# A two-layer diffusion step on one core: gate blocks, final norm, first weights and operand placement

## The chip, the core and the metric

One core of a Trainium2 chip runs the whole program. The metric is the time of one execution in microseconds (us) on the device; lower is better. The five engines are PE (matrix multiply; its weight loads are listed as PEld), DVE (vector), ACT (scalar activations), POOL (GpSimd) and SP, which issues most DMAs here. Each engine runs its own instructions strictly in the written order and waits at semaphores for the others.

## The reference

Two token groups go through the same two layers: 256 latent tokens (conditioned by `c`, reading cached context keys and values) and 128 context tokens (conditioned by `c_ctx`). D is 1024, there are 8 heads of 128, and the FFN width is 2816. Everything is float32.

```python
def run_layer(x, cond, l, ctx_kv, use_rope):
    mod = silu(cond) @ w_mod[l] + b_mod[l]              # 9 vectors of 1024
    sh1, sc1, gt1, sh2, sc2, gt2, sh3, sc3, gt3 = split(mod, 9)
    h = rmsnorm(x, g_norm[l, 0]) * (1 + sc1) + sh1
    x = x + 0.5 * gt1 * swiglu(h, ffn1_w13[l], ffn1_w2[l])
    h = rmsnorm(x, g_norm[l, 1]) * (1 + sc2) + sh2
    m, k_state, v_state = mixer(h, l, ctx_kv, use_rope)
    x = x + gt2 * m
    h = rmsnorm(x, g_norm[l, 2]) * (1 + sc3) + sh3
    return x + 0.5 * gt3 * swiglu(h, ffn2_w13[l], ffn2_w2[l])

def mixer(h, l, ctx_kv, use_rope):
    z, q, k, v, gates = split(h @ w_in[l])
    u, vv = split(gelu(z))                              # gating unit
    a = u * (w_spatial[l] @ rmsnorm(vv, gain) + b_spatial[l])   # 128x128 mixing, 4 groups
    o = softmax(q1 k1) v - lam * softmax(q2 k2) v       # per head, rope on latents
    b = rmsnorm(o, subln_gain[l]) * (1 - lam_init)
    return (sigmoid(g_a) * (a @ w_branch_a) + sigmoid(g_b) * (b @ w_branch_b)) @ w_out

y = rmsnorm(x after two layers, g_final)                # for both groups
```

## The kernel before

All 384 tokens sit side by side in the free dimension: `x` is 128 partitions x 8 tiles (`dt`) x 384 tokens. A projection is computed as three matmuls per 128x128 weight tile (`mm3`, lines 233 to 235): weights and activations are each split into a rounded high part and the rest (`whi`/`wlo`, `S_hi`/`S_lo`), and hi*hi, lo*hi and hi*lo are added in PSUM. ACT writes the high part of each weight chunk of 128x1024 (line 181), DVE the low part (line 184); SP loads the chunks into seven `raw` buffers (line 150).

The order of the program is written by a small planner: a list of *jobs*, each consuming weight chunks in order. A *column job* (`col_job`) is 24 matmuls with 384 moving columns (386 where the un-normed `u` is used, whose last two columns carry the shift vector); a *token-major job* (`tokmajor_job`, lines 394 to 396) is 18 matmuls with 512 moving columns. At the start of every job with weights one entry of the list `bg` is run (`run_bg(1)`), and attention interleaves its phases with matmuls by the table `ORDER` (`F3` means three steps of a job, `X2` means phase x of the unit two back).

Three places are touched.

*The gate* (`push_sgu`, pushed just before the q and k jobs of head 0). `sgu_norm` computes 1/rms of the gated half (POOL does the power and the refinement steps), `sgu_scale(j)` scales token tile j (DVE, line 762), and `sgu_block(cb)` does three mixing matmuls (PE, line 773) into one PSUM tile `tp`, of which there is a single buffer, and then evacuates it on DVE and ACT (lines 777, 780, 414, 417). The next block's matmuls can start when line 777 has read `tp`. The jobs that follow are q0, k0 and eight token-major jobs for v (v0 to v7); with v0 to v3 go steps of the next modulation vectors, DVE work at lines 443, 445, 451 and 460.

*The start* (`start_group`). Before the first projection, layer 0's first shift and scale vectors are computed in four quarters: `products(q)` is 32 small matmuls (line 302), `finish(q)` two transposes (line 317) and a few DVE operations, after which `make(kt)` writes the normed activations of tiles 2q and 2q+1 (lines 556, 561, 564). `warm(n)` issues n matmuls on a tile of ones with no reader (line 336).

*The end*. After the last FFN, `update_x` (line 628) and `norm_sq` (lines 508, 509) finish the eighth tile of x, `norm_stats` sums squares on PE (line 532), `rsqrt` runs on POOL and DVE, `norm_bcast` spreads the result over partitions (lines 545 to 549), and eight DVE operations (line 1127) write y, each followed by a DMA from SP (line 1130).

Where the tiles lie: the allocator gives every tile a multiple of 32 bytes in each partition. In the built program before the change, `x`, `t`, `raw` and the activation slots S0 and S2 to S6 start 32 bytes past a multiple of 128, and S1, S7, all `whi` and `wlo` 96 bytes past one. A row of 384 numbers is 1536 bytes, 12 times 128; a row of `u` is 1544 bytes, so its eight rows start 8 bytes further along each time.

Of the kernel before, what the change touches and what calls it, by code (L numbers as in the profile page):

```python
# [26 lines left out]
RAW_BUFS = 7  # L27
PER_HEAD = 27
LO_LAG = 4
ORDER = [(c[0], int(c[1:])) for c in "S0 F1 B0 T1 F3 E0 C0 O2 F4 P1 F1 X2".split()]  # L30
W_BUFS = 4
WARM = (28, 5, 10)
TINY = {"yq": 2, "yv": 2, "ys": 2, "yl": 2, "yb": 3, "y2": 4, "yo": 4, "ye": 4, "yc": 4}

SH1, SC1, GT1, SH2, SC2, GT2, SH3, SC3, GT3 = range(9)
TOK = ((1, 0, 256), (0, 256, 384))
# [5 lines left out]
def hybrid_step(  # L42
# [29 lines left out]
    bmod = cp.tile([P, DEPTH, 9, KD], F32, name="bmod")  # L72
    gnorm = cp.tile([P, DEPTH, 3, KD], F32, name="gnorm")
    sgain = cp.tile([P, DEPTH, KD], F32, name="sgain")
    sublng = cp.tile([P, DEPTH], F32, name="sublng")
    gfin = cp.tile([P, KD], F32, name="gfin")
    neglam = cp.tile([P, DEPTH], F32, name="neglam")
    modT = cp.tile([P, DEPTH, 9, KD, 2], F32, name="modT")
    amod = cp.tile([P, 3, KD, 2], F32, name="amod")

# [207 lines left out]
    def start_group(keys, rhs, evacs, make):  # L288
# [42 lines left out]
        junk = pp.tile([P, P], F32, tag="tp", name="tp")  # L331

        def warm(n):

            for _ in range(n):
                T.matmul(junk, lhsT=ones, rhs=ones, start=True, stop=True)

        def gen(c):
            n = len(keys)
            nst["h"] = duo(role["Y"])  # L340
            warm(WARM[0])
            norm_stats()
            products(0)
            warm(WARM[1])
            norm_bcast()
            finish(0)
            warm(WARM[2])
            for i in range(2):
                split_upto(c + i)
                make(i)  # L350
                run_later(99)
            split_upto(c + n - 1)
            run_later(99)
            ws = [split_of.pop(c + i) for i in range(n)]
            pss = [ps_mm() for _ in range(n)]
            r_hi, r_lo = rhs()
            for q in range(4):
                seq = [(i, kt) for kt in (2 * q, 2 * q + 1) for i in range(n)]
                if q == 3:
                    seq = [(i, kt) for i in range(n) for kt in (6, 7)]  # L360
                for e, (i, kt) in enumerate(seq):
                    if q < 3 and e == (5, 1, 1)[q]:
                        products(q + 1)
                    if q < 3 and e == (7, 3, 3)[q]:
                        finish(q + 1)
                        make(2 * q + 2)
                        make(2 * q + 3)
                    sl = slice(kt * P, (kt + 1) * P)
                    hi, lo = ws[i]
                    mm3(pss[i][:, :NT], hi[:, sl], lo[:, sl], r_hi[:, kt, :], r_lo[:, kt, :], kt == 0, kt == KD - 1)  # L370
                    if kt == KD - 1:
                        evacs[i](pss[i][:, :NT])
# [218 lines left out]
    def make_u(l, i, kt):  # L591

        if kt == 0:
            nst["u"] = tuple(slot(2 * role["Y"] + n, [P, KD, NU], F32R) for n in range(2))
        u_hi, u_lo = nst["u"]
        for n, s0, s1 in TOK:
            S.activation(
# [28 lines left out]
    def update_x(l, pc, dt, ps, after):  # L626
        for n, s0, s1 in TOK:
            V.scalar_tensor_tensor(  # L628
                out=x[:, dt, s0:s1], in0=ps[:, s0:s1], scalar=modT[:, l, pc, dt, n:n + 1],
                in1=x[:, dt, s0:s1], op0=ALU.mult, op1=ALU.add)  # L630
        norm_sq(dt)
        if after is not None:
            make_u(*after, dt)


    def ffn(l, i, w13, w2, mods, after, n13):
# [83 lines left out]
    def mixer(l, mods, after):  # L720
# [362 lines left out]
    with tc.manual_schedule():  # L1083
# [39 lines left out]
        norm_stats()
        norm_bcast()
        y = slot(0, [P, KD, NT])
        for dt in range(KD):
            V.scalar_tensor_tensor(
                out=y[:, dt, :], in0=x[:, dt, :], scalar=gfin[:, dt:dt + 1], in1=nst["rb"],
                op0=ALU.mult, op1=ALU.mult)
            nc.sync.dma_start(out=a["y"][:, dt, :], in_=y[:, dt, :])  # L1130


# [77 lines left out]
```

## Time and profile before

| | |
|---|---|
| median of 3 runs | 1936.64 us (1936.42 to 1937.65) |
| profiled execution | 1935.43 us, of which the span from first to last instruction is 1933.7 us |
| PE busy | 1908.7 us, 99% of the span |
| matmuls at lines 233, 234 and 235 | 3136 each: 2816 with 384 columns, 320 with 386 |
| DVE, ACT, POOL busy | 1323.3, 795.2, 248.9 us |
| DMA | 308.71 MB, mean 160 GB/s |
| granted PE clock | 0.995 mean |

Times in the profile count from the span's start. In a row of the timeline the columns are: start in us, length in us, engine, line of the kernel, operation, output<-inputs, size, how many equal instructions the row merges, and in brackets how long the engine had been idle and who ended that. PE's pipelined matmuls overlap, so their lengths are latencies; the distance between starts is their rate. In the table of windows the columns are the stretch, its length, the busy time and number of instructions of each engine, the granted PE clock, the DMA share and GB/s.

### The profile page before, as it was taken

To read this page: it belongs to the slowest core of one execution; us is meant where nothing else is said; L and a number is where in the kernel's file an instruction comes from. 1 tells how busy PE (TensorE), PEld (TensorE's weight loads), DVE (VectorE), ACT (ScalarE), POOL (GpSimd) and SP (SyncE) were. 2 spreads that over 40 slices of the span, in tenths; PEclk is the share of its full clock that TensorE was granted. 3 is DMA by queue.
4 is the path that set the end of the run, shared out by engine and by line. 5 is a ranking of instruction groups with operands and counts; after the bars stand their busy time and mean duration, and the time that the engine had idled before them with its cause. 6 is when DMAs were issued, how large, how long until landed. Compare 5 with 4: busy or idle time off the path is not lost.

```text
span 1933.7 us, 28616 instructions
## 1 busy us (share of the span) xinstructions
PE 1908.7 (99%) x10992; PEld 1839.8 (95%) x10992; DVE 1323.3 (68%) x2016; ACT 795.2 (41%) x1435; POOL 248.9 (13%) x527
## 2 busy tenths in 40 slices
PE   8999999999999999999999999999999999999997
PEld 6999999878899999999999999998898999999997
DVE  4677885777666668778768779668677456655533
ACT  3433334536653344333334333344565534433321
POOL 0000003203431022000040000050134300400000
PEclk9999999999999999999999999999999999999998
DMA  8566664643334435566536556545333333354430
GB/s 312 198 196 200 215 210 131 208 144 110 99 100 156 151 115 190 192 199 214 197 99 222 196 191 226 171 136 191 121 103 97 113 120 124 115 172 157 153 109 34
DMA packets 92154, 308.71 MB, mean 160 GB/s; under 512 B 10864, under 2 KB 18416, under 8 KB 91248
## 3 DMA queue, kind: packets, MB, share of 16 engines
q1 hardware_dynamic: 91584, 306.76, 48.4%
q8 instruction: 87, 1.43, 0.3%
q14 instruction: 51, 0.42, 0.1%
q10 hardware_dynamic: 432, 0.11, 0.0%
HBM read 303.16 MB, written 3.67 MB: 159 GB/s over the span
## 4 chain that ended last, share of the span: by engine, by line
PE 82%; issue 13%; DVE 3%; POOL 1%; DMA 1%; ACT 1%; POOLq 0%; DVEq 0%; ACTq 0%
PE mm L233 24%; PE mm L234 23%; PE mm L235 23%; PE mm L394 2%; PE mm L396 2%; PE mm L395 2%; PE sc L943 2%; PE mm L992 1%; DVE wlo L184 1%; PE tp L976 1%; PE sc L302 0%; DMA S<-in_w_mod 0%; POOL t L578 0%; PE tp L773 0%; POOL t L576 0%
## 5 line engine op out<-in xcount | busy, mean ns | idle before, releaser
L233 PE MATMUL mm<-S,whi 128*128 128x384 f32 (+1 forms) x3136 | 1073.8, 342 | 2.3 <-ACT S L561 2.3
L234 PE MATMUL mm<-S,wlo 128*128 128x384 f32 (+1 forms) x3136 | 1053.5, 336 | 3.7 <-DVE wlo L184 3.6
L235 PE MATMUL mm<-S,whi 128*128 128x384 f32 (+1 forms) x3136 | 1050.7, 335 | 0.0
L184 DVE TENSOR_TENSOR wlo<-raw,whi 128x1024 fp32r<-128x1024 f32 x424 | 520.0, 1227 | 241.6 <-ACT whi L181 241.0
L233 PEld LDWEIGHTS mm<-S,whi 128*128 128x128 f32 x3136 | 589.9, 188 | 24.7 <-issue 18.7
L234 PEld LDWEIGHTS mm<-S,wlo 128*128 128x128 f32 x3136 | 588.6, 188 | 5.4 <-DVE wlo L184 5.1
L235 PEld LDWEIGHTS mm<-S,whi 128*128 128x128 f32 x3136 | 589.2, 188 | 0.4 <-DVE S L564 0.4
L181 ACT ACTIVATE whi<-raw 128x1024 fp32r<-128x1024 f32 x424 | 445.0, 1051 | 186.6 <-PE mm L235 112.8
L445 DVE SCALAR_TENSOR_TENSOR acc<-raw,scond,acc 128x1024 f32<-128x1024 f32 x224 | 277.1, 1278 | 0.0
L414 ACT ACTIVATE S<-t 128x384 fp32r<-128x384 f32 x144 | 73.9, 522 | 332.6 <-DVE t L672 241.2
L515 POOL TENSOR_TENSOR yr<-yv,nhalf 128x3 f32<-128x3 f32 x9 | 7.7, 856 | 1344.8 <-DVE yv L535 1269.8
L417 DVE TENSOR_TENSOR S<-t,S 128x384 fp32r<-128x384 f32 x144 | 83.7, 588 | 34.5 <-ACT S L414 34.5
L672 DVE TENSOR_TENSOR t<-t,mm 128x384 f32<-128x384 f32 x76 | 42.0, 553 | 77.9 <-PE mm L235 77.8
L653 ACT ACTIVATE t<-mm 128x384 f32<-128x384 f32 x76 | 37.3, 490 | 137.7 <-PE mm L235 137.7
L394 PE MATMUL mm<-whi,S 128*128 128x512 f32 x192 | 77.4, 403 | 0.0
L396 PE MATMUL mm<-whi,S 128*128 128x512 f32 x192 | 75.2, 392 | 0.0
L395 PE MATMUL mm<-wlo,S 128*128 128x512 f32 x192 | 75.1, 391 | 0.0
L508 ACT ACTIVATE t<-x 128x384 f32<-128x384 f32 x45 | 23.4, 524 | 109.5 <-DVE x L628 109.5
L578 POOL TENSOR_SCALAR t<-t,amod,modT 128x256 f32<-128x256 f32 x80 | 67.0, 846 | 4.2
L628 DVE SCALAR_TENSOR_TENSOR x<-mm,modT,x 128x256 f32<-128x256 f32 x96 | 35.5, 411 | 33.1 <-PE mm L235 32.9
L576 POOL TENSOR_TENSOR t<-x,rb 128x384 f32<-128x384 f32 x40 | 49.0, 1224 | 28.9 <-ACT rb L549 20.3
L955 ACT ACTIVATE e<-sc,ym 128x384 f32<-128x384 f32 (+1 forms) x96 | 47.9, 507 | 6.7 <-DVE ym L946 6.4
(138 smaller groups left out, 1189.1 us busy)
## 6 DMA issues: line engine op xcount, KB each, us to landing
raw<-in_ffn_w SPq DMA_DIRECT2D x264, 512.0 KB, 4.4
raw<-in_w_mod SPq DMA_DIRECT2D x132, 512.0 KB, 4.7
raw<-in_w_in SPq DMA_DIRECT2D x112, 512.0 KB, 3.9
raw<-in_w_branch_a SPq DMA_DIRECT2D x16, 512.0 KB, 3.6
raw<-in_w_branch_b SPq DMA_DIRECT2D x16, 512.0 KB, 3.7
raw<-in_w_out SPq DMA_DIRECT2D x16, 512.0 KB, 3.7
S<-in_w_mod SPq DMA_DIRECT2D x6, 1024.0 KB, 10.4
x<-in_x SPq DMA_DIRECT2D x4, 384.0 KB, 4.3
```

What stands on the lines that cost most here:

```text
L181: S.activation(out=hi, in_=raw, func=AF.Copy)
L184: V.tensor_tensor(out=lo, in0=raw, in1=hi.bitcast(F32), op=ALU.subtract)
L233: T.matmul(ps, lhsT=w_hi, rhs=r_hi, start=first, stop=False)
L234: T.matmul(ps, lhsT=w_lo, rhs=r_hi, start=False, stop=False)
L235: T.matmul(ps, lhsT=w_hi, rhs=r_lo, start=False, stop=last)
L394: T.matmul(ps, lhsT=l_hi[:, kt, ts_], rhs=hi[:, sl], start=first, stop=False)
L395: T.matmul(ps, lhsT=l_hi[:, kt, ts_], rhs=lo[:, sl], start=False, stop=False)
L396: T.matmul(ps, lhsT=l_lo[:, kt, ts_], rhs=hi[:, sl], start=False, stop=last)
L414: S.activation(out=dst_hi, in_=src, func=AF.Copy)
L417: V.tensor_tensor(out=dst_lo, in0=src, in1=dst_hi.bitcast(F32), op=ALU.subtract)
L445: V.scalar_tensor_tensor(out=acc[n], in0=raw, scalar=s, in1=acc[n], op0=ALU.mult, op1=ALU.add)
L578: G.tensor_scalar(out=t[:, s0:s1], in0=t[:, s0:s1], scalar1=amod[:, i, kt, n:n + 1], scalar2=modT[:, l, pc_sh, kt, n:n + 1], op0=ALU.mult, ...
```

## The change

It does five things. (1) In `push_sgu` an empty entry goes first, the three scales become one entry, and the first block gets an entry of its own, so blocks come one job later. (2) In `start_group` the first two weight chunks are split before the first activations are made, the two later groups of `warm` go, and `products(q + 1)` and `finish(q + 1)` of the first quarter come two and one tile triples earlier. (3) The final norm gets a function of its own: y is first written as x times the gain by ACT while the last FFN still runs, the squares of seven tiles are summed inside the FFN's last output tile, the eighth tile's squares are added after it, `warm` fills PE's waits, and the multiply with 1/rms is shared by DVE (three pairs of tiles, straight from PSUM) and POOL (two tiles), with DMAs from SP and ACT. (4) In `ORDER` phase x moves from the end of a round to the next round, behind the transposes. (5) Two 2-column tiles become one, some tiny pools change their number of buffers, and `u` is allocated with rows of 388 numbers (1552 bytes), of which 386 are used as before. In the built program `x`, `t`, `raw`, `whi`, `wlo`, `at`/`acc`/`rb` and all S slots then start at a multiple of 128 bytes; `qf`, `kf` and `vc` start 32 bytes past one and `e` 64 bytes past one; rows of `u` start 16 bytes further along each time.

```diff
-ORDER = [(c[0], int(c[1:])) for c in "S0 F1 B0 T1 F3 E0 C0 O2 F4 P1 F1 X2".split()]
+ORDER = [(c[0], int(c[1:])) for c in "S0 F1 B0 T1 X3 F3 E0 C0 O2 F4 P1 F1".split()]
-TINY = {"yq": 2, "yv": 2, "ys": 2, "yl": 2, "yb": 3, "y2": 4, "yo": 4, "ye": 4, "yc": 4}
+TINY = {"yq": 2, "yv": 2, "ys": 2, "yl": 2, "yb": 3, "y2": 4, "yo": 4, "ye": 4, "yc": 2, "ym": 4, "yz": 4}
...
-    sublng = cp.tile([P, DEPTH], F32, name="sublng")
+    per_layer = cp.tile([P, 2 * DEPTH], F32, name="per_layer")
+    sublng = per_layer[:, 0:DEPTH]
     gfin = cp.tile([P, KD], F32, name="gfin")
-    neglam = cp.tile([P, DEPTH], F32, name="neglam")
+    neglam = per_layer[:, DEPTH:2 * DEPTH]
...
-            warm(WARM[0])
+            warm(28)
             norm_stats()
+            split_upto(c)
             products(0)
-            warm(WARM[1])
+            run_later(99)
+            split_upto(c + 1)
             norm_bcast()
             finish(0)
-            warm(WARM[2])
-            for i in range(2):
-                split_upto(c + i)
-                make(i)
-                run_later(99)
+            make(0)
+            run_later(99)
+            make(1)
...
-                    if q < 3 and e == (5, 1, 1)[q]:
+                    if q < 3 and e == (3, 1, 1)[q]:
                         products(q + 1)
-                    if q < 3 and e == (7, 3, 3)[q]:
+                    if q < 3 and e == (6, 3, 3)[q]:
                         finish(q + 1)
...
-            nst["u"] = tuple(slot(2 * role["Y"] + n, [P, KD, NU], F32R) for n in range(2))
+            nst["u"] = tuple(slot(2 * role["Y"] + n, [P, KD, NU_ROW], F32R)[:, :, 0:NU] for n in range(2))
...
         def push_sgu():
+            bg.append(lambda: None)
             bg.append(sgu_norm)
-            bg.append(lambda: (sgu_scale(0), sgu_scale(1)))
-            bg.append(lambda: (sgu_scale(2), sgu_block(0)()))
-            for cb in range(1, KD):
+            bg.append(lambda: [sgu_scale(j) for j in range(3)])
+            for cb in range(KD):
                 bg.append(sgu_block(cb))
...
+    def final():
+        warm(8)
+        final_sums(1)
+        r = rsqrt(nst["v"], 3, V)
+        warm(9)
...
+        S.activation(out=rb, in_=ps, func=AF.Copy)
+        y = nst["y"]
+        for dt in range(2):
+            G.tensor_tensor(out=y[:, dt, :], in0=y[:, dt, :], in1=rb, op=ALU.mult)
+            nc.scalar.dma_start(out=a["y"][:, dt, :], in_=y[:, dt, :])
+        for dt in range(2, KD, 2):
+            ys = y[:, dt:dt + 2, :]
+            V.tensor_tensor(out=ys, in0=ys, in1=ps.unsqueeze(1).to_broadcast([P, 2, NT]), op=ALU.mult)
+            nc.sync.dma_start(out=a["y"][:, dt:dt + 2, :], in_=ys)
```

In the order of instructions three places matter. First DVE at the gate, from the rope of head 0's q (lines 793 to 796 before, 847 to 850 after; `S_3301`/`S_3285` is the gated half, `yr` 1/rms). Before:

```order
L796 TENSOR_TENSOR qf<-qf,t 128x256
L762 TENSOR_SCALAR S_3301<-S_3301,yr 128x1024 x2
L184 TENSOR_TENSOR wlo<-raw,whi 128x1024
L793 STREAM_SHUFFLE t<-kf 128x256
L794 TENSOR_TENSOR t<-t,sin_t 128x256
L795 TENSOR_TENSOR kf<-kf,cos_t 128x256
L796 TENSOR_TENSOR kf<-kf,t 128x256
L762 TENSOR_SCALAR S_3301<-S_3301,yr 128x1024
L777 SCALAR_TENSOR_TENSOR t<-tp,sgain,bb 128x384
L780 TENSOR_TENSOR t<-t,S_2912 128x384
L417 TENSOR_TENSOR S_3528<-t,S_3527 128x384
L184 TENSOR_TENSOR wlo<-raw,whi 128x1024
```

And after, on the same engine and place:

```order
L850 TENSOR_TENSOR qf<-qf,t 128x256
L811 TENSOR_TENSOR yv<-ys 128x3
L812 TENSOR_SCALAR yv<-yv 128x3
L185 TENSOR_TENSOR wlo<-raw,whi 128x1024
L847 STREAM_SHUFFLE t<-kf 128x256
L848 TENSOR_TENSOR t<-t,sin_t 128x256
L849 TENSOR_TENSOR kf<-kf,cos_t 128x256
L850 TENSOR_TENSOR kf<-kf,t 128x256
L816 TENSOR_SCALAR S_3285<-S_3285,yr 128x1024 x3
L185 TENSOR_TENSOR wlo<-raw,whi 128x1024
L445 TENSOR_REDUCE red<-acc 128x32 x2
L831 SCALAR_TENSOR_TENSOR t<-tp,sgain,bb 128x384
```

All three scales now stand together behind the rope of k, and the first block's evacuation stands a job later, behind a weight split and a modulation step. On PE the first block stands between two token-major jobs (512 columns) instead of between k0 and v0.

Second, DVE at the start, from the sum of squares to the second activation tile. Before:

```order
L545 TENSOR_SCALAR t<-ident,yr 128x128 x3
L319 TENSOR_REDUCE yq<-sc 128x8
L323 TENSOR_TENSOR modT<-yq,bmod 128x4
L327 SCALAR_TENSOR_TENSOR amod<-modT,gnorm 128x4
L323 TENSOR_TENSOR modT<-yq,bmod 128x4
L556 SCALAR_TENSOR_TENSOR t<-x,amod,rb 128x256
L556 SCALAR_TENSOR_TENSOR t<-x,amod,rb 128x128
L564 SCALAR_TENSOR_TENSOR S_152<-t,modT,S_151 128x256
L564 SCALAR_TENSOR_TENSOR S_152<-t,modT,S_151 128x128
L184 TENSOR_TENSOR wlo<-raw,whi 128x1024
```

After:

```order
L185 TENSOR_TENSOR wlo<-raw,whi 128x1024
L539 TENSOR_SCALAR t<-ident,yr 128x128 x3
L320 TENSOR_REDUCE yq<-sc 128x8
L324 TENSOR_TENSOR modT<-yq,bmod 128x4
L328 SCALAR_TENSOR_TENSOR amod<-modT,gnorm 128x4
L324 TENSOR_TENSOR modT<-yq,bmod 128x4
L550 SCALAR_TENSOR_TENSOR t<-x,amod,rb 128x256
L550 SCALAR_TENSOR_TENSOR t<-x,amod,rb 128x128
L558 SCALAR_TENSOR_TENSOR S_150<-t,modT,S_149 128x256
L558 SCALAR_TENSOR_TENSOR S_150<-t,modT,S_149 128x128
L185 TENSOR_TENSOR wlo<-raw,whi 128x1024
```

The first chunk's low part moved ahead of the broadcast; the second chunk's low part stands where the first one's stood.

Third, the last instructions of PE. Before:

```order
L235 MATMUL mm<-S_17066,whi 128x384
L532 MATMUL ms<-ones,acc 128x2 x3
L546 MATMUL ms<-t,ones 128x128
L547 MATMUL ms<-t,ones 128x256
L1202 UNCONDITIONAL_BRANCH
```

After:

```order
L236 MATMUL mm<-S_17050,whi 128x384
L635 MATMUL tp<-ones 128x128 x8
L653 MATMUL ms<-ones,t 128x2 x3
L635 MATMUL tp<-ones 128x128 x9
L674 MATMUL ms<-t,ones 128x128
L675 MATMUL ms<-t,ones 128x256
L1248 UNCONDITIONAL_BRANCH
```

The sums of the first seven tiles are no longer among them: they stand inside the last output tile of the FFN, and matmuls on ones stand ahead of the sums and ahead of the broadcast.

More of the change, by code (lines that the diff above doesn't have):

```diff
@@ L20 @@
 NU = NT + 2
+NU_ROW = NT + 4
 DEPTH = 2
@@ L29 @@
 LO_LAG = 4
-ORDER = [(c[0], int(c[1:])) for c in "S0 F1 B0 T1 F3 E0 C0 O2 F4 P1 F1 X2".split()]
+ORDER = [(c[0], int(c[1:])) for c in "S0 F1 B0 T1 X3 F3 E0 C0 O2 F4 P1 F1".split()]
 W_BUFS = 4
-WARM = (28, 5, 10)
-TINY = {"yq": 2, "yv": 2, "ys": 2, "yl": 2, "yb": 3, "y2": 4, "yo": 4, "ye": 4, "yc": 4}
+TINY = {"yq": 2, "yv": 2, "ys": 2, "yl": 2, "yb": 3, "y2": 4, "yo": 4, "ye": 4, "yc": 2, "ym": 4, "yz": 4}
 SH1, SC1, GT1, SH2, SC2, GT2, SH3, SC3, GT3 = range(9)
@@ L329, in finish @@
                         in1=gnorm[:, 0, 0, dts].unsqueeze(2).to_broadcast([P, 2, 2]), op0=ALU.add, op1=ALU.mult)
[L331 to L336, printed above, removed]
         def gen(c):
@@ L630, in update_x, with warm, final_part @@
                 in1=x[:, dt, s0:s1], op0=ALU.mult, op1=ALU.add)
-        norm_sq(dt)
         if after is not None:
+            norm_sq(dt)
             make_u(*after, dt)
+        else:
+            final_part(dt)
+    def warm(n):
+        junk = pp.tile([P, P], F32, tag="tp", name="tp")
+        for _ in range(n):
+            T.matmul(junk, lhsT=ones, rhs=ones, start=True, stop=True)
+    def final_part(dt):
+        if dt == 0:
+            nst["y"] = slot(2 * role["Y"], [P, KD, NT])
+        if dt < KD - 1:
+            norm_sq(dt)
+        else:
+            nst["last"] = tmp()
+            S.activation(out=nst["last"], in_=x[:, dt, :], func=AF.Square)
+        S.activation(out=nst["y"][:, dt, :], in_=x[:, dt, :], func=AF.Copy, scale=gfin[:, dt:dt + 1])
@@ new lines, in final_sums @@
+    def final_sums(n):
+        if n == 0:
+            nst["st"] = pp.tile([P, 2, 3, 2], F32, tag="ms", name="ms")
+        for j in range(3):
+            sl = slice(j * P, (j + 1) * P)
+            T.matmul(
+                nst["st"][:, n, j, :], lhsT=nst["acc" if n == 0 else "last"][:, sl], rhs=ones[:, 0:2],
+                start=True, stop=True)
+        if n == 0:
+            nst["v"] = tiny(3, "yv")
+            V.tensor_scalar(
+                out=nst["v"], in0=nst["st"][:, 0, :, 0], scalar1=1.0 / D, scalar2=EPS, op0=ALU.mult, op1=ALU.add)
+        else:
+            V.scalar_tensor_tensor(
+                out=nst["v"], in0=nst["st"][:, 1, :, 0], scalar=1.0 / D, in1=nst["v"], op0=ALU.mult, op1=ALU.add)
@@ new lines, in final @@
+    def final():
[3 more added lines that the diff above has]
+        warm(9)
+        ps = pp.tile([P, NT], F32, tag="ms", name="ms")
+        dg = tmp()
+        for j in range(3):
+            sl = slice(j * P, (j + 1) * P)
+            V.tensor_scalar(out=dg[:, sl], in0=ident, scalar1=r[:, j:j + 1], scalar2=None, op0=ALU.mult)
+        T.matmul(ps[:, 0:P], lhsT=ones, rhs=dg[:, 0:P], start=True, stop=True)
+        T.matmul(ps[:, P:NT], lhsT=ones, rhs=dg[:, P:NT], start=True, stop=True)
+        rb = sp.tile([P, NT], F32, tag="at", name="rb")
+        S.activation(out=rb, in_=ps, func=AF.Copy)
[7 more added lines that the diff above has]
+            nc.sync.dma_start(out=a["y"][:, dt:dt + 2, :], in_=ys)
@@ L708, in gen @@
                     mm3(ps[:, :NT], hi[:, sl], lo[:, sl], a_hi, a_lo, kt == 0, kt == NFF - 1)
+                    if after is None and (dt, kt) == (KD - 1, 12):
+                        final_sums(0)
                     yield
@@ L1121, in hybrid_step @@
         run_later(99)
[L1123 to L1130, printed above, removed]
+        final()
 def _cols(w, n0, n):
```

## The prediction, made before the changed kernel ran

> **What bounds the kernel now.** I read the page's first lines, then the chain that ended last, then the distance between matmul starts, then each place where PE waits.
>
> ```profile
> span 1933.7 us, 28616 instructions
> PE 1908.7 (99%) x10992; PEld 1839.8 (95%) x10992; DVE 1323.3 (68%) x2016; ACT 795.2 (41%) x1435; POOL 248.9 (13%) x527
> PE 82%; issue 13%; DVE 3%; POOL 1%; DMA 1%; ACT 1%; POOLq 0%; DVEq 0%; ACTq 0%
> ```
>
> PE is the bound: the chain is PE nearly everywhere, so only two things can shorten the span: a shorter distance between matmuls, or the removal of a PE wait. The distance first, in the timeline of PE, column jobs of layer 0 and, below, jobs on `u`:
>
> ```profile
> 599.76 0.34 PE L233 MATMUL mm<-S,whi 128*128 128x384 f32 x1
> ...
> 602.88 0.34 PE L233 MATMUL mm<-S,whi 128*128 128x384 f32 x1
> 718.25 0.34 PE L233 MATMUL mm<-S,whi 128*128 128x386 f32 x1
> ...
> 719.83 0.34 PE L233 MATMUL mm<-S,whi 128*128 128x386 f32 x1
> ...
> 720.36 0.34 PE L233 MATMUL mm<-S,whi 128*128 128x386 f32 x1
> ...
> 722.48 0.34 PE L233 MATMUL mm<-S,whi 128*128 128x386 f32 x1
> ```
>
> Eighteen matmuls of 384 columns take 3.12 us, 173.3 ns each; 24 of 386 columns take 4.23 us, 176.3 ns each. No wait is in this: it is the stream itself, 8448 matmuls of the first width and 960 of the second. The waits are in three places, and the change touches all three.
>
> **The gate.** Timeline of DVE, PE and POOL in layer 0, then PE in layer 1:
>
> ```profile
> 387.07 1.41 DVE L762 TENSOR_SCALAR S<-S,yr 128x1024 f32<-128x1024 f32 x2
> 388.89 0.61 PE L773 MATMUL tp<-ws,S 128*128 128x128 f32 x4
> 391.22 0.74 DVE L762 TENSOR_SCALAR S<-S,yr 128x1024 f32<-128x1024 f32 x1
> 392.02 0.49 PE L773 MATMUL tp<-ws,S 128*128 128x128 f32 x2 [2.53 <-DVE S L762]
> 395.30 1.22 DVE L184 TENSOR_TENSOR wlo<-raw,whi 128x1024 fp32r<-128x1024 f32 x1 [0.39 <-ACT whi L181]
> 396.51 0.83 PE L773 MATMUL tp<-ws,S 128*128 128x128 f32 x6
> 415.64 0.61 DVE L777 SCALAR_TENSOR_TENSOR t<-tp,sgain,bb 128x384 f32<-128x384 f32 x1
> 416.31 0.94 PE L773 MATMUL tp<-ws,S 128*128 128x128 f32 x6
> 383.67 0.85 POOL L515 TENSOR_TENSOR yr<-yv,nhalf 128x3 f32<-128x3 f32 x1 [37.65 <-DVE yv L758]
> 386.09 0.32 POOL L520 TENSOR_TENSOR yr<-ye,yr 128x3 f32<-128x3 f32 x1
> 1331.34 0.61 PE L773 MATMUL tp<-ws,S 128*128 128x128 f32 x4
> 1334.47 0.49 PE L773 MATMUL tp<-ws,S 128*128 128x128 f32 x2 [2.53 <-DVE S L762]
> ```
>
> The first block's six records take 3.62 us (388.89 to 392.51) where an unhindered block takes 0.83: 2.8 us lost to the third scale, which stands behind the rope of k; the same in layer 1. After the change the scales begin where the third one begins now, 391.22 (1/rms needs 2.74 us on POOL, from about 387.5, so it is there by 390.3), and end at 391.22 + 0.74 + 2 x 0.67 = 393.3. PE comes to the first block after v0, 18 matmuls or 4.24 us (392.27 to 396.51) after 388.89, at 393.1, and the first two scales are ready then: no wait. Layer 1 keeps the whole 2.8 us.
>
> In layer 0 DVE is late next. From the weight split at 395.30 to the end of line 777 at 416.25 it works through 20.95 us of splits, block evacuations and modulation steps, and that end releases PE's block at 416.31. The order of the change has the same work behind the scales, but one block evacuation fewer in front of it, so it starts at 393.3 and releases PE at the same job (v5) at 414.3. PE alone would be there near 412.9, so about 1.4 us come back as a wait, and the layer gains 2.0. Sum of the gate: 2.0 + 2.8 = 4.8 us. Bounds: 3.6 if DVE is 1.2 us later (one more split ahead), 5.6 if nothing comes back. The eighth block now goes with the first job of attention, where DVE gets some 2.3 us of its work ahead of the first maximum; the transposes that need that unit come a round later, which covers it; uncovered it would cost at most those 2.3 us, twice.
>
> **The start.** Timeline of ACT, DVE and PE, and a window for the clock:
>
> ```profile
> 17.60 0.49 ACT L549 ACTIVATE rb<-ms 128x384 f32<-128x384 f32 x1 [1.68 <-PE ms L547]
> 18.58 0.75 DVE L556 SCALAR_TENSOR_TENSOR t<-x,amod,rb 128x256 f32<-128x256 f32 x2
> 19.95 0.44 PE L233 MATMUL mm<-S,whi 128*128 128x384 f32 x1
> 20.30 1.22 DVE L184 TENSOR_TENSOR wlo<-raw,whi 128x1024 fp32r<-128x1024 f32 x1
> 23.16 3.49 DVE L184 TENSOR_TENSOR wlo<-raw,whi 128x1024 fp32r<-128x1024 f32 x3
> 28.60 2.27 PE L302 MATMUL sc<-S,scond 128*32 128x256 f32 x32
> 31.95 0.38 PE L317 MATMUL sc<-ident,t 128*128 128x128 f32 x2
> 34.43 0.44 PE L233 MATMUL mm<-S,whi 128*128 128x384 f32 x1 [1.57 <-ACT S L561]
> 25.00:28.00 3.00, 2.56 (x9) 1.84 (x8) 1.65 (x2) 0.00 (x0) 0.00 (x0) 0.65 0.99 408
> ```
>
> PE waits here for DVE's low parts, which end at 26.65. The first one moves ahead of the broadcast, where DVE is idle, but the broadcast then waits for it, so the first activation comes about when it does now (18.6 to 18.8). Behind it DVE has three splits instead of four, and ACT makes chunks 2 and 3 only after both activation tiles, so the last low part is still there near 26.5. What moves is PE's order: the second quarter's products stand before the fourth chunk's triple and can run from about 25.7 instead of 28.60. At full clock they take some 1.9 us; nine matmuls (1.6) follow, and the transposes come at 29.4 instead of 31.95, a gain of up to 2.5 us, which 34.43 and all behind it keeps. Against it stands the clock. The 15 warming matmuls go, and PE is nearly empty from 17.8 to 25.5; in the window 25 to 28 the granted clock is 0.65 already with them. If the half clock lasts until the products have run, they take about twice as long and the gain is 0.9. I take 1.2, near the slow end since the warming goes; ends 0 and 2.7.
>
> [...]
>
> **The end.** Timeline of the last microseconds, and a group of the page:
>
> ```profile
> 1917.89 0.34 PE L235 MATMUL mm<-S,whi 128*128 128x384 f32 x1
> 1919.05 0.52 ACT L508 ACTIVATE t<-x 128x384 f32<-128x384 f32 x1 [10.93 <-DVE x L628]
> 1919.60 0.56 DVE L509 TENSOR_TENSOR acc<-acc,t 128x384 f32<-128x384 f32 x1 [0.59 <-ACT t L508]
> 1920.21 1.36 PE L532 MATMUL ms<-ones,acc 128*128 128x2 f32 x6 [1.98 <-DVE acc L509]
> 1921.86 0.85 POOL L515 TENSOR_TENSOR yr<-yv,nhalf 128x3 f32<-128x3 f32 x1 [245.00 <-DVE yv L535]
> 1924.33 1.06 PE L547 MATMUL ms<-t,ones 128*128 128x256 f32 x2
> 1925.43 0.49 ACT L549 ACTIVATE rb<-ms 128x384 f32<-128x384 f32 x1 [5.86 <-PE ms L547]
> 1925.96 4.32 DVE L1127 SCALAR_TENSOR_TENSOR S<-x,gfin,rb 128x384 f32<-128x384 f32 x8 [1.94 <-ACT rb L549]
> 1926.60 4.20 SPq L1130 DMA_DIRECT2D out_y<-S  x8
> L576 POOL TENSOR_TENSOR t<-x,rb 128x384 f32<-128x384 f32 x40 | 49.0, 1224 | 28.9 <-ACT rb L549 20.3
> ```
>
> The addition at 1919.60 goes; the warming holds PE until about 1919.9, so the sums start 0.3 earlier, and at full clock they take about half of 1.36: together 0.95. The power and the DVE steps stay. The broadcast at full clock saves about 0.45 of its 1.06. DVE multiplies straight from PSUM, which saves the copy's 0.5, but its first DMA waits for a pair, two times 0.54: the first issue moves from 1926.60 to about 1925.1. From the first issue to the end are 7.1 us now, in which 1.57 MB go out; three producers (POOL's two tiles at 1.22 each lie beside) feed the same bytes no slower, so I keep 7.1: a gain of 1.5 to 2.3, the latter if larger rows leave faster. Back goes 0.6 to 0.7 for the six small records now inside the FFN. Net 1.2; ends 0.5 and 2.
>
> **Edits at nothing.** Phase x keeps its one transpose per unit beside other small matmuls, before beside the scores, now beside phase t; its result is needed after attention. Fewer tiny buffers: each is read again within its round. ACT's early y is beside the FFN, in which ACT is idle (10.93 us before 1919.05). The placement: all 384-column operands start 32 bytes past a multiple of 64 now, so no row shows the new case for them. The nearest are the rows of `u`: its fifth row (719.83 to 720.36) has its high part at 64 and its low part at 0 past a multiple of 128, and its three matmuls take 0.53 us, the mean of the eight. A start at such a multiple gains nothing there. I take 0 for 8448 matmuls; for the 960 on `u` anything between 173.3 and 179 ns, -3 to +2 us.
>
> **The rivals.** (A) Alignment is the stream's limit. If operands were fetched in pieces of 128 bytes, 1536 bytes from a shifted start touch 13 pieces and from an aligned start 12; 173.3/13 is 13.3 ns a piece, and 8448 matmuls would save up to 112 us: 1815 to 1880. For it: 386 columns touch 13 pieces either way, so the rows of `u` don't exclude it. Against: two more columns cost 3 ns, which it does not explain. (B) Slower: with every start in one phase, moving and stationary reads collide, and the uneven 176.3 ns of `u` becomes the rule for 384 columns: 3 ns x 8448 = 25 us, 1954. It decides from 1 ns per matmul (8 us). Against: the 18 matmuls from 599.76 read S0 and S1, or S6 and S7, whose low part already stands in the weights' phase, 96 past a multiple of 128, and their mean is still 173.3. (C) The gate's wait moves on: DVE is late in layer 1 too, or the eighth block holds up attention's first unit; the gate is worth 1.5 and the sum about 4: 1932.6. (D) Nothing gained, the three waits return elsewhere: 1936.
>
> [...]
>
> **How the numbers follow.** 4.8 + 1.2 + 1.2 = 7.2 us. The profiled execution took 1935.43, its span 1933.7; the median of the runs shown is 1936.64, 1.2 above it, and I subtract from the median: 1929.4. Adding the good ends (5.6, 2.7, 2, 3 on `u`) gives 1923.3; the bad ends (3.6, 0, 0.5, and 2 lost on `u`) give 1934.5. Eight times in ten I expect 1923.5 to 1933.5. Chances: forecast 0.76, A 0.08, B 0.05, C 0.08, D 0.03. A difference under 0.2% (3.9 us) is about what a measurement of this kernel can't tell from none. Faster: nearly all of the forecast, A, and half of C, 0.86; same: 0.09; slower: B, 0.05.
>
> **What would show it.** The first block of the gate in either layer without an idle time on PE; in layer 0 a wait of 1 to 2 us for line 777's successor near v5. At the start the second products near 25 to 26 us and a lower granted clock around 20 to 29. At the end the first output DMA some 7 us after the last FFN matmul instead of 8.7. The 384-column distance still 173.3 ns: if it is not, the forecast is wrong, whatever the waits do.

## The result and the profile after

The change made the kernel slower: 1949.93 us (median of 4 runs, 1949.48 to 1950.89) against 1937.14 us for the kernel before in the same session. The ratio is 1.0068, 95% interval 1.0055 to 1.0080. The profiled execution took 1949.48 us. The page's span, its busy times and the engines of the chain that ended last:

```profile
span 1947.7 us, 28627 instructions
PE 1929.3 (99%) x11002; PEld 1859.0 (95%) x11002; DVE 1323.8 (68%) x2011; ACT 794.2 (41%) x1443; POOL 249.7 (13%) x529
PE 97%; DVE 2%; DMA 1%; ACT 1%; issue 0%; DVEq 0%; SPq 0%
```

PE's busy time rose by 20.6 us (1908.7 to 1929.3), and the part of the span in which PE was not busy fell by 6.6 (25.0 to 18.4). So the waits went about as forecast, and something else took three times as much. The granted clock is 0.995 in both. That leaves the distance between matmuls. PE's timeline, column jobs of layer 1 (`L234` to `L236` are lines 233 to 235 of before):

```profile
1800.08 0.34 PE L234 MATMUL mm<-S,whi 128*128 128x384 f32 x1
...
1802.71 0.34 PE L234 MATMUL mm<-S,whi 128*128 128x384 f32 x1
1802.88 0.34 PE L235 MATMUL mm<-S,wlo 128*128 128x384 f32 x1
1803.07 0.33 PE L236 MATMUL mm<-S,whi 128*128 128x384 f32 x1
1803.23 0.34 PE L234 MATMUL mm<-S,whi 128*128 128x384 f32 x1
```

Eighteen matmuls take 3.15 us where they took 3.12, and a triple is no longer even: 0.17, 0.19, 0.16 us. From the starts of all uninterrupted triples (some 2600; from one start of the first line to the next) the mean was 520.0 to 520.6 ns before and is 526.5 now on slots S0/S1 and S6/S7, 528 on S2 to S5. By the mean distance within unbroken runs of 20 or more: 174.21 to 176.45 ns at 384 columns, times 8448 is 18.9 us; 230.3 to 233.7 at 512 columns, times 576 is 1.9; 177.3 to 177.7 at 386, times 960 is 0.4. Together 21.2, close to the rise of 20.6 in busy time.

The three places of waits. The gate, PE in layer 0 and 1 and DVE in layer 0 (the first four rows are PE's):

```profile
397.17 0.83 PE L827 MATMUL tp<-ws,S 128*128 128x128 f32 x6
413.99 0.50 PE L388 MATMUL mm<-whi,S 128*128 128x512 f32 x1 [0.49 <-ACT S L880]
418.28 0.94 PE L827 MATMUL tp<-ws,S 128*128 128x128 f32 x6 [0.54 <-DVE t L831]
1347.60 0.83 PE L827 MATMUL tp<-ws,S 128*128 128x128 f32 x6
395.31 2.07 DVE L816 TENSOR_SCALAR S<-S,yr 128x1024 f32<-128x1024 f32 x3
417.62 0.61 DVE L831 SCALAR_TENSOR_TENSOR t<-tp,sgain,bb 128x384 f32<-128x384 f32 x1
```

The first block runs in 0.83 us without an idle time in either layer. In layer 0 a wait of 0.54 stands near v5, as forecast in kind, and one that the forecast did not have, for ACT's evacuation, stands ahead of it.

The start, first in windows (PE's busy time first, the granted clock third from the end):

```profile
20.00:23.00 3.00, 2.52 (x6) 1.64 (x6) 2.54 (x5) 0.94 (x4) 0.00 (x0) 0.50 1.01 421
23.00:26.00 3.00, 1.26 (x3) 0.75 (x3) 2.49 (x4) 2.17 (x3) 0.00 (x0) 0.50 1.01 429
26.00:29.00 3.00, 3.00 (x26) 1.24 (x29) 0.62 (x1) 0.00 (x0) 0.00 (x0) 0.50 1.00 412
```

and PE's timeline there:

```profile
26.48 3.64 PE L303 MATMUL sc<-S,scond 128*32 128x256 f32 x32
32.22 0.38 PE L318 MATMUL sc<-ident,t 128*128 128x128 f32 x2
```

The second products start 2.1 us earlier (26.48 against 28.60) but take 3.64 us at a granted clock of 0.50, against 2.27 before; their transposes come at 32.22, no earlier than before (31.95).

The end, PE, ACT, DVE and SP:

```profile
1933.67 0.34 PE L236 MATMUL mm<-S,whi 128*128 128x384 f32 x1
1939.59 0.49 ACT L677 ACTIVATE rb<-ms 128x384 f32<-128x384 f32 x1 [3.73 <-PE ms L675]
1940.11 2.68 DVE L684 TENSOR_TENSOR S<-S,ms 128x768 f32<-128x768 f32 x3 [1.31 <-ACT rb L677]
1941.09 2.11 SPq L685 DMA_DIRECT2D out_y<-S  x3
```

From the last FFN matmul to the first output DMA: 7.42 us, against 8.71.

### The profile page after: what moved, and what is told of

It reads as the page before. It is cut to its first block, busy times and chain, and to the rows that moved or that the text cites. A ratio compares the mean times of both kernels' runs of the same rounds, so it can differ in the third digit from the quotient of the medians.

```text
span 1947.7 us, 28627 instructions
## 1 busy us (share of the span) xinstructions
PE 1929.3 (99%) x11002; PEld 1859.0 (95%) x11002; DVE 1323.8 (68%) x2011; ACT 794.2 (41%) x1443; POOL 249.7 (13%) x529
## 4 chain that ended last, share of the span: by engine, by line
PE 97%; DVE 2%; DMA 1%; ACT 1%; issue 0%; DVEq 0%; SPq 0%
PE mm L234 29%; PE mm L235 29%; PE mm L236 28%; PE mm L389 2%; PE mm L390 2%; PE mm L388 2%; PE sc L997 2%; PE mm L1046 1%; PE tp L1030 1%; DMA raw<-in_ffn_w 0%; DVE wlo L185 0%; PE tp L827 0%; PE sc L303 0%; PE ms L1069 0%; ACT whi L182 0%; PE tp L635 0%
## 5 line engine op out<-in xcount | busy, mean ns | idle before, releaser
L234 PE MATMUL mm<-S,whi 128*128 128x384 f32 (+1 forms) x3136 | 1077.5, 344 | 5.1 <-ACT S L555 3.9
L235 PE MATMUL mm<-S,wlo 128*128 128x384 f32 (+1 forms) x3136 | 1069.3, 341 | 0.6 <-DVE wlo L185 0.6
L236 PE MATMUL mm<-S,whi 128*128 128x384 f32 (+1 forms) x3136 | 1049.6, 335 | 0.0
L234 PEld LDWEIGHTS mm<-S,whi 128*128 128x128 f32 x3136 | 588.7, 188 | 28.0 <-issue 19.1
L236 PEld LDWEIGHTS mm<-S,whi 128*128 128x128 f32 x3136 | 589.7, 188 | 0.4 <-DVE S L558 0.4
L999 DVE TENSOR_REDUCE ym<-sc 128x2 f32<-128x768 f32 (+1 forms) x48 | 37.3, 776 | 25.4 <-PE sc L997 25.1
```

What stands on the lines that cost most here:

```text
L234: T.matmul(ps, lhsT=w_hi, rhs=r_hi, start=first, stop=False)
L235: T.matmul(ps, lhsT=w_lo, rhs=r_hi, start=False, stop=False)
L236: T.matmul(ps, lhsT=w_hi, rhs=r_lo, start=False, stop=last)
```

## The experiments

In all of them d is the start of a weight tile minus the start of an activation tile in the partition, counted by 256 bytes unless said otherwise; d_hi is taken to the high activations, d_lo to the low ones. All rows of 384 columns (1536 bytes) and all weight tiles (512 bytes) keep d within a job.

### Which placement, and is it the placement at all

Four kernels. The first is the changed kernel with everything from `nhalf` on 32 bytes lower (an unused constant goes):

```diff
-    epst = cp.tile([P, 1], F32, name="epst")
```

> The changed kernel with x, t, raw, whi, wlo and every activation slot 32 bytes lower in each partition (all 96 past a multiple of 128, so 32 past a multiple of 64, as every matmul operand stood before the change, counted by 64); the order of instructions is that of the changed kernel. Placement theory: in the changed kernel three matmuls of 384 columns take 526.5 ns against 520 before, 8448/3 triples x 6.5 ns = 18.3 us, some 2 us more at 512 columns; both go, and the time is 1949.9 - 20 = 1930 (1927 to 1933), the triple 520 ns. Rival, same phase: the stream is slow because activations and weights start at the same place counted by 128 bytes; they still do here, so 1950. Rival, order: the new order of instructions and its waits cost the time, wherever the operands lie; 1950.

Measured 1949.84 us, ratio to before 1.0061 (1.0046 to 1.0076); triples 526.5 and 528.0, the same values slot by slot as in the changed kernel. The page shows PE as busy as there (1929.8 against 1929.3). So alignment to 64 or 128 bytes by itself is not what costs: no operand of the matmuls with 384 and 512 columns starts at a multiple of 64 here.

```profile
span 1947.9 us, 28627 instructions
PE 1929.8 (99%) x11002; PEld 1858.6 (95%) x11002; DVE 1323.6 (68%) x2011; ACT 794.0 (41%) x1443; POOL 248.9 (13%) x529
```

The second takes a 96-byte set of tiny tiles ahead of the first weight tile, so only the weights move:

```diff
             raw = raw_of[key]
+            if st["split"] == 0:
+                tiny(2, "yb")
             hi = sp.tile([P, 1024], F32R, tag="whi", name="whi", bufs=W_BUFS)
```

> The changed kernel with only the weights moved: whi and wlo start 96 bytes past a multiple of 128 (32 past a multiple of 64), the activation slots stay at multiples of 128. If the stationary operand's start decides: fast, 1930. If the moving operand's start decides: unchanged, 1950. If the two must differ in phase: fast, 1930. If the order of instructions costs the time: 1950.

Measured 1931.04 us, ratio 0.9966 (0.9953 to 0.9978); triples 520.2 to 521.1. The order of instructions is the changed kernel's; 96 bytes on the weights give back 18.9 us of the median, and the page shows them in PE's busy time:

```profile
span 1928.3 us, 28627 instructions
PE 1910.5 (99%) x11002; PEld 1839.6 (95%) x11002; DVE 1321.6 (69%) x2011; ACT 793.9 (41%) x1443; POOL 249.5 (13%) x529
```

The third has the first edit and a pad of 32 bytes ahead of the weights, so only the activations (with `x`, `t`, `raw`) move:

> The changed kernel with only x, t, raw and the activation slots moved by 32 bytes (to 96 past a multiple of 128); whi and wlo stay at multiples of 128. If the moving operand's start decides (at 384 columns these slots are the moving side): fast, 1930. If the stationary operand's start decides: unchanged, 1950, but at 512 columns, where the activations are the stationary side, 231 instead of 233.7 ns. If the two must differ in phase: 1930. If the order of instructions costs the time: 1950.

Measured 1952.11 us, ratio 1.0073 (1.0058 to 1.0088); triples 527.7 and 530.0. Both theories of a single operand's place fall (places counted by 128 here, as in these expectations): with activations at 96 it is slow here and in the first run, with weights at 96 it is slow in the first and fast in the second. "Must differ" falls too. What the first run and the changed kernel share is the distance.

The fourth is the kernel before with part (5) alone, every address as in the changed kernel:

```diff
+NU_ROW = NT + 4
...
+            for tag in ("whi", "wlo"):
+                sp.tile([P, 1024], F32R, tag=tag, name=tag, bufs=W_BUFS)
             finish(0)
```

> The kernel before with part (5) of the change alone: every address of x, t, raw, whi, wlo and the activation slots is that of the changed kernel, the order of instructions that of the kernel before. Placement theory: 1937 + 18.3 + 2 = 1957 (1954 to 1960), triples of 526 ns. If the other four parts cost the time: 1937, triples of 520 ns.

Measured 1956.81 us, ratio 1.0097 (1.0082 to 1.0112): 19.1 us slower than before in the same session, by the placement alone. PE's busy time, with the old order of instructions, is 22.5 us above that of before (1908.7):

```profile
PE 1931.2 (99%) x10992; PEld 1861.0 (95%) x10992; DVE 1325.8 (68%) x2016; ACT 795.3 (41%) x1435; POOL 248.6 (13%) x527
```

### The distance by itself

A kernel that computes nothing of the reference: one tile `m` of activations, one tile `w` of weights, and PE runs the triple 32 times per case with shifted starts, while the other engines are idle (the heart of it; `kd` is 8 and `step` 384 in the cases with 384 columns):

```python
for kt in range(kd):
    hi, lo = wh // 4 + kt * P, 1152 + wl // 4 + kt * P
    r_hi, r_lo = mh // 4 + kt * step, 3200 + ml // 4 + kt * step
    seq += [(hi, r_hi), (lo, r_hi), (hi, r_lo)]
...
T.matmul(ps[:, :n], lhsT=w[:, s:s + P], rhs=m[:, r:r + n], start=e == 0, stop=e == len(seq) - 1)
```

> A measurement of the disputed cost by itself; nothing of the reference is computed. One tile m holds high and low activations, one tile w high and low weights, both at addresses that are multiples of 512, lows a multiple of 512 behind the highs; PE runs the kernel's triple (hi*hi, lo*hi, hi*lo; rows of 1536 bytes, weight tiles of 512 bytes) 32 times per case, nothing else runs. The cases shift the starting bytes; d is weights minus activations. Theory, relative phase: what counts is d, not where both lie; four runs agree with this for d counted by 128 (0 in the changed kernel and in the one with both moved: 526.5; 32: 527.7; 64 before the change: 520; 96: 520.2). So per triple d = 0 and 32 give 526 to 528, d = 64 and 96 give 520, d = 0 with both shifted by 8 to 64 gives 526 again, and the values between fall between. By 256 rather than 128: d and d + 128 differ. Rival, absolute places of the weights (the four runs have whi at 224 or 224 by 256 where fast, 96 or 128 where slow): shifting both changes the time. Which pair collides: if high activations against either weight, shifting only whi or only wlo by 64 takes away half of the 6.5 ns; if the low activations count, shifting them alone changes it. By the distance between starts at d = 64, 384 columns cost 173.3 ns; if that is a floor of the array's own, widths around 384 follow a straight line through it, and no case lies below 520.

Its PE timeline merges each case of 96 matmuls into one row; the second column is the case's whole length. The rows are, in this order, d = 0, 32, 64, 96, 128, 144, 160, 256, 384; then both tiles shifted by 16 and by 32 with d = 0; then d = 40:

```profile
49.58 16.92 PE L82 MATMUL mm<-m,w 128*128 128x384 f32 x96
...
83.64 16.91 PE L82 MATMUL mm<-m,w 128*128 128x384 f32 x96
...
117.40 16.89 PE L82 MATMUL mm<-m,w 128*128 128x384 f32 x96
...
151.38 16.90 PE L82 MATMUL mm<-m,w 128*128 128x384 f32 x96
...
185.12 17.15 PE L82 MATMUL mm<-m,w 128*128 128x384 f32 x96
...
202.25 17.27 PE L82 MATMUL mm<-m,w 128*128 128x384 f32 x96
...
219.49 17.20 PE L82 MATMUL mm<-m,w 128*128 128x384 f32 x96
...
321.53 16.92 PE L82 MATMUL mm<-m,w 128*128 128x384 f32 x96
...
355.29 17.14 PE L82 MATMUL mm<-m,w 128*128 128x384 f32 x96
...
406.14 17.10 PE L82 MATMUL mm<-m,w 128*128 128x384 f32 x96
...
423.22 16.90 PE L82 MATMUL mm<-m,w 128*128 128x384 f32 x96
...
491.01 17.50 PE L82 MATMUL mm<-m,w 128*128 128x384 f32 x96
```

16.9 us is a triple of 520 ns, 17.10 one of 527, 17.15 one of 528, 17.50 one of 540; "free" below means 520. The distance counts by 256, not by 128 as my theory had it: 0 and 256 are free, 128 and 384 cost the same. The case with d_hi = 128 and d_lo = 0 gave starts 175, 181.7 and 170 ns apart, the uneven triple of the changed kernel. So the slow stream needs no other engine: PE's weights and moving columns alone make it. Moving both leaves the time as it is for 8, 32 and 64 bytes, but 16 bytes cost (17.10), so d does not tell all.

Beside it ran the changed kernel with the weights 64 bytes further on (`tiny(8, "yq")` at the place of the second run's edit):

> The changed kernel with only whi and wlo moved by 64 bytes: weights 64 past a multiple of 128, activations at multiples of 128, every operand still at a multiple of 64. If multiples of 64 as such were the trouble: 1950. If the distance between weights and activations counts, and 64 is the distance that the kernel before had between its weights and its high activations: triples of 520 ns, 512 columns at 230.5, 1930 (1927 to 1932).

Measured 1935.4 us, ratio 0.9990 (0.9980 to 1.0000): a miss by 5 us. About 1.2 of them lie in the start (the 61st matmul of the split stream comes at 46.24 us, against 45.00 in the second run); the rest is in the stream. S2 to S5 had triples of 520, S0/S1 and S6/S7 a mixture with means of 523.2 and 522.4. Counted by 256 these slots stand at (d_hi, d_lo) = (192, 64), a pair that no kernel had had. So I measured the pairs, with the same bare kernel, three groups per case:

> The same bare measurement as the phase run, three groups of triples per case, nothing of the reference computed. d_hi is the weights' start minus the high activations', d_lo the weights' minus the low activations', both counted by 256 in steps of 32: 64 pairs as column triples (384 columns), 64 as token-major triples (512 columns, activations stationary), and 386 columns with rows of 1544 and 1552 bytes. Theory (distance by 256): the pairs that the kernels have give their kernels' numbers: (64,0) and (192,192) 520, (128,0) 526.5, (128,128) 527 to 528, (160,32) 527.7, (160,160) 530, (224,96) and (224,224) 520, (192,64) 522 to 523; bad pairs have d_hi 128 or 160. For 512 columns (0,0) is the best at about 680 and most others near 700. Rival (absolute places after all): pairs and kernels disagree. With only whi or only wlo at 128: between 520 and 527. One weight tile for all three matmuls at distance 128 or 40: if it is weight loads that collide with moving reads, still slow.

Nanoseconds per triple at 384 columns, from the first and last starts of a case with the first six matmuls left out; rows are d_hi, columns d_lo:

```
d_hi    0     32     64     96    128    160    192    224
  0   520.0  523.4  527.0  526.6  526.7  519.9  522.0  520.0
 32   523.2  520.0  526.7  529.8  520.0  520.5  526.7  523.5
 64   520.0  526.9  530.0  526.6  526.5  523.3  520.4  520.1
 96   524.3  526.6  526.8  520.0  523.3  529.9  522.6  529.8
128   526.9  526.3  526.8  523.5  528.0  526.5  525.9  526.6
160   526.6  533.3  526.8  526.7  528.8  530.0  526.5  526.7
192   521.8  520.2  524.4  523.3  520.1  526.7  520.0  526.6
224   522.4  526.7  526.6  519.9  526.4  526.5  523.5  519.9
```

No pair with d_hi at 128 or 160 is free, and none with d_lo at 64; elsewhere it hangs on both, so that d_hi alone, as the expectation had it, does not mark the bad pairs. One of the two weight tiles at 128 with all else at 0 is enough (526.8 for the high one, 526.3 for the low one), and three matmuls on one weight tile at 128 take 528.0, at 40 540.0. At 512 columns (0,0) is best with 680 ns a triple; most pairs give 690 to 702. The table is no perfect law: (64,64) gives 530.0 here and 520 in the phase run, with the very same shifts. The pairs of S2 to S5, one distance for both, agree with the kernels: 528.0 at (128,128) in both, 530.0 at (160,160), 520 at (192,192). Against the kernels (S0/S1 and S6/S7; triple in the kernel, in the table, and at 512 columns in kernel and bare):

| kernel | d_hi, d_lo | triple | table | 512 columns | time, us |
|---|---|---|---|---|---|
| before | 64,0 and 192,128 | 520.6, 520.2 | 520.0, 520.1 | 691 (688.5 at 64,0) | 1937 |
| after; both moved | 128,0 | 526.5 | 526.9 | 701 (700.7) | 1950 |
| weights at 96 | 224,96 | 520.2 | 519.9 | 695 (699.9) | 1931 |
| activations at 96 | 160,32 | 527.7 | 533.3 | 700.5 (700.0) | 1952 |
| weights at 64 | 192,64 | 523.2, 522.4 | 524.4 | 695.4 (695.6) | 1935 |

### The start's clock

On the second run's kernel, the two groups of warming put back:

```diff
             products(0)
+            warm(5)
             run_later(99)
...
             finish(0)
+            warm(10)
             make(0)
```

> The changed kernel with the weights at 96 past a multiple of 128 (1931.0 us), and at the start the two groups of 5 and 10 warming matmuls put back behind the first products and the first transposes. Theory (the clock took the start's gain): with them the granted clock, 0.50 from 20 to 29 us in the run without them, stays near 1 until about 25; the second products, 3.49 us long at 26.3, take 2.3 to 2.6, and the 61st matmul of the stream, at 45.00 now and 45.50 before the change, comes at 44.0 to 44.4. Rival (low parts and activations, not the clock, set it): 45.0 again. Against it: warming may stand in front of the first triple and make it later by up to 0.5.

Measured 1930.57 us in one run. Windows, and PE's row of the second products, first here and then in the second run's kernel without the warming:

```profile
20.00:23.00 3.00, 2.00 (x9) 1.02 (x8) 2.69 (x6) 0.94 (x4) 0.00 (x0) 1.00 1.01 421
23.00:26.00 3.00, 1.35 (x3) 0.79 (x3) 2.51 (x4) 1.97 (x3) 0.00 (x0) 0.58 1.01 429
```

```profile
26.27 3.64 PE L305 MATMUL sc<-S,scond 128*32 128x256 f32 x32
26.34 3.49 PE L305 MATMUL sc<-S,scond 128*32 128x256 f32 x32
```

A miss: the clock holds until 23.5 us and then falls ahead of the products, which take 3.64 us, no less than without the warming (3.49); the 61st matmul comes at 45.30 instead of 45.00. Then with five more where PE waits for a high part:

```diff
                 for e, (i, kt) in enumerate(seq):
+                    if q == 0 and e == 2:
+                        warm(5)
                     if q < 3 and e == (3, 1, 1)[q]:
```

> As the run before, with 5 more warming matmuls ahead of the third tile triple, where PE waits 1.17 us for a high part. Theory: the clock then stays near 1 through the second products as well, they take some 1.9 us, and the 61st matmul comes at 43.5 to 43.9. Rival: the clock is already up without them, no further gain; or the third triple is delayed by up to 0.5.

The same two views:

```profile
20.00:23.00 3.00, 2.48 (x16) 1.82 (x15) 2.54 (x5) 0.94 (x4) 0.00 (x0) 1.00 1.00 423
23.00:26.00 3.00, 1.74 (x12) 1.21 (x10) 2.41 (x4) 2.25 (x4) 0.00 (x0) 1.00 1.01 429
```

```profile
26.16 1.93 PE L305 MATMUL sc<-S,scond 128*32 128x256 f32 x32
```

The clock stays at 1.00, the products take 1.93 us, and the 61st matmul comes at 43.28, 1.72 earlier; one run took 1928.38 us. In the first of these two runs the clock fell although PE's longest idle time between 20 and 26 us is 1.56 us. How little work lets it fall is not shown. With PE busy for 2.00 and 1.35 us of two windows of 3 us it fell within the second, with 2.48 and 1.74 it did not, but the kernel before held it to 25.93 us with less:

```profile
20.00:23.00 3.00, 1.19 (x5) 0.61 (x4) 2.69 (x7) 1.89 (x4) 0.00 (x0) 1.00 1.01 421
23.00:26.00 3.00, 1.23 (x5) 0.91 (x6) 3.00 (x4) 1.64 (x2) 0.00 (x0) 0.99 1.02 423
26.00:29.00 3.00, 2.91 (x12) 1.77 (x14) 0.65 (x1) 0.00 (x0) 0.00 (x0) 0.50 0.99 403
```

The clock's changes stand 6.83 us apart in the first run (23.50 and 30.33) and 3.41, half of that, in the kernel before (25.93 and 29.34), so where these steps begin may count as well as the work.

### A placement from the table, and the worst one

Rows of `u` at 1544 bytes again, the three groups of warming, and small tiles between the slots, so that every d is 0:

```diff
+            h_hi = slot(2 * role["Y"], [P, KD, NT], F32R)
+            take(("ym", 2), ("yc", 1))
+            h_lo = slot(2 * role["Y"] + 1, [P, KD, NT], F32R)
+            take(("yz", 2), ("yv", 3))
```

(`take` makes one tile of each named pool; tiles of other pools stand likewise behind S6 and S7.)

> The changed kernel with the three groups of warming matmuls of the last run, rows of u at 1544 bytes again, and small tiles put between the slots so that every activation slot and every weight tile starts at the same place counted by 256 bytes (a distance of 0 everywhere; in the changed kernel it is 128 for the high activations). Theory (distance by 256): by the pairs run, 384 columns at (0,0) take 520.0 ns a triple, 512 columns 680 against 695 with the weights at 96, 386 columns 528.5 against 531.5: 192 x 15 + 320 x 3 ns = 3.8 us less than the warmed run with the weights at 96 (1928.4), so 1924.6 (1923 to 1926.5). Rival (alignment as such is bad): all starts are still multiples of 128 bytes, as in the changed kernel; 1948. Rival (the bare measurement doesn't carry over to 512 columns beside other engines' work): 1928.

Measured 1925.89 us (5 runs, 1925.67 to 1926.14), ratio to before 0.9943 (0.9930 to 0.9955): the fastest version, below both kernels. Triples 520.3 to 520.6, 512 columns 681 ns, every operand of these at a multiple of 256. The same with the weights 160 bytes further on (a pad of 40 numbers ahead of `whi`):

> The kernel of the run before with the weights alone 160 bytes further on, so that every distance is 160, the worst of the steps of 32 in the pairs run. Theory: triples of 530.0 ns at 384 columns (2646 whole ones were seen, 2816 in all), 702.8 at 512, 530.4 at 386: 2816 x 10 + 192 x 22.6 + 320 x 1.9 ns = 33 us above the run before, so 1957.5 (1954 to 1960), slower than the changed kernel. Rival (only multiples of 128 collide): as fast as the run before, 1925.

Measured 1955.28 us, ratio 1.0094 (1.0078 to 1.0109). Triples 530.0 in all slots, 512 columns 703.6 ns, as the table had them. The page's busy times with every d at 0, and then with every d at 160:

```profile
PE 1909.5 (99%) x11042; PEld 1842.8 (96%) x11042; DVE 1321.5 (69%) x2011; ACT 794.4 (41%) x1443; POOL 249.4 (13%) x529
```

```profile
PE 1939.6 (99%) x11042; PEld 1871.0 (96%) x11042; DVE 1324.2 (68%) x2011; ACT 794.5 (41%) x1443; POOL 248.5 (13%) x529
```

Nothing in the code differs but the pad of 160 bytes; PE is busy 30.1 us longer in the second.

## Why the prediction was wrong

**The step that failed: the price of the placement.** "I take 0 for 8448 matmuls" was 2.24 ns each, 18.9 us, plus 1.9 us on 576 matmuls of 512 columns, which the sum did not carry at all. The evidence for 0 was the fifth row of `u`, whose operands stand at multiples of 64 and cost no more than the other rows. That row speaks of where an operand lies; what costs is how far two operands lie apart, which the change moved for all columns at once (d_hi from 64 or 192 to 128). The prediction's own last test, the 384-column distance, is what showed it.

**Rival B came nearest**, with 3 ns and 1954 us where 2.24 ns and 1950 were measured. That moving and stationary reads collide, as it has it, is not shown; that their distance sets the pace is. "Every start in one phase" is not the condition, however: with every d at 0 the stream is the fastest of all. The argument used against it, that the low parts already stood in the weights' phase, was true and beside the point: d_lo was 0 or 128, and the pairs (64,0) and (192,128) are free. It was the high parts that came to 128.

**Rival A fell**: a start at a multiple of 128 saves nothing; three kernels with all starts there gave 1926, 1950 and 1957.

**The waits were right in kind, and a little less in size.** The run with only the weights moved has the changed order of instructions and the old stream, so its matmuls can be set against those of before, one by one (start of the k-th split matmul, us):

| k | before | weights at 96 | difference | what lies between |
|---|---|---|---|---|
| 60 | 45.50 | 45.00 | -0.50 | the start |
| 1920 | 380.55 | 380.13 | -0.43 | |
| 1980 | 395.12 | 391.27 | -3.85 | first block of the gate, layer 0 |
| 2118 | 433.01 | 431.20 | -1.82 | the waits of layer 0, and the eighth block |
| 6840 | 1306.27 | 1304.52 | -1.75 | |
| 7140 | 1381.41 | 1377.37 | -4.04 | the gate, layer 1 |
| 9900 | 1903.50 | 1899.22 | -4.28 | |
| 9960 | 1913.91 | 1910.29 | -3.62 | the early sums of the end |
| span | 1933.7 | 1928.3 | -5.4 | the end |

The gate: 1.4 in layer 0 (2.0 forecast) and 2.3 in layer 1 (2.8), 3.7 against 4.8; in layer 0 the wait near v5 was smaller than the 1.4 forecast, but an idle time of 0.5 for ACT's evacuation came beside it. The start: 0.5 by this pair of traces, against 1.2. But this moment moves between runs: in the other traces with the new order and no added warming the 61st matmul comes at 45.63 to 46.24 us (45.83 in the changed kernel itself), and in the run with the old order and the new placement at 46.26, of which the slower stream explains less than 0.2. So without warming a gain of the start is not shown; the earlier products ran wholly at half clock (0.50), the slow case that I had put at 0.9. With the clock held the 61st matmul comes at 43.28, 42.76 and 43.36 in three runs, 2.1 to 2.7 us earlier than before, near the good end of 2.7. The end: 0.66 given back in the sums and 1.8 gained behind them, 1.1 net against 1.2; the multiply straight from PSUM did not save ACT's copy, since DVE's first one still waits for it (1.31 us, ended by `rb`), and the rest came from the last DMAs (6.6 us from the first issue to the end instead of 7.1). **Rivals C and D** fell: the gate kept 3.7, not 1.5, and layer 1 has no new wait at the block. Together 5.4 us of 7.2 by the span, the doubtful 0.5 of the start included; the medians of that run's session differ by 6.7.

**Why these distances cost time stays open.** The runs show that PE alone does it, that d by 256 sorts most cases, and that a bare measurement foretells a kernel within about 1 ns per triple for most pairs, but (192,64) was off by up to 2, (160,32) was 533.3 there and 527.7 in the kernel, a common shift by 16 bytes costs 6.7 ns at d = 0, and (64,64) had two values. What ran just before a case may count too; that was not tried.

## What to carry to other kernels

Where PE's stream is the bound, the place of its operands is part of the tuning: look at the distance between matmul starts before any wait, since 96 bytes of small tiles ahead of the weights moved this kernel by 1% (1950 to 1931 us). "Aligned" is not the property to ask for (with all starts at multiples of 128 this kernel took 1926, 1950 and 1957 us); measure the triple of the kernel in a bare loop over the distance between stationary and moving tiles, and lay the slots out by that table. An edit that reorders work and also moves addresses should be timed in two parts, or a gain of 5 to 7 us hides behind a loss of 19.

## What the runs showed of the hardware that I had not expected

The spread between the best and the worst distance in steps of 32 bytes is 520 to 533 ns per triple at 384 columns and 680 to 706 at 512. And the free distance itself is not proportional to the columns. From the phase run, 380 and 416 columns at d = 64 (96 matmuls each) and 512 columns at d = 0 (72):

```profile
719.12 16.89 PE L82 MATMUL mm<-m,w 128*128 128x380 f32 x96
...
822.32 18.17 PE L82 MATMUL mm<-m,w 128*128 128x416 f32 x96
...
918.73 16.60 PE L82 MATMUL mm<-m,w 128*128 128x512 f32 x72
```

380 columns cost as much as 384 (16.89 us). Triples of 480, 520, 560 and 680 ns at 352, 384, 416 and 512 columns are 160.0, 173.3, 186.7 and 226.7 ns a matmul: each is the columns plus 32, divided by 2.4 per ns (160 more columns took 66.7 ns more). The line holds for these widths at a free distance, not for every width: 368, 400 and 448 columns, run at d = 64 alone, took 506.6, 550.0 and 606.7 ns where it gives 500, 540 and 600. And 386 columns, two more than 384, pay for more than two (528 against 520 ns a triple with every d at 0).
